# Where the vector engine's side work stands at the seams of a two-layer encoder: sums, weight splits, transposes and the loads of x

## The chip, the cores and the metric

The kernel runs on one core of a Trainium2 chip. The core has a matrix engine (TensorE, PE in the profile; PEld is its loading of the stationary operand), a vector engine (VectorE, DVE), an activation engine (ScalarE, ACT), GpSimd (POOL) and a queue engine that only issues transfers (SyncE, SP). The metric is the device time of one execution in microseconds, the median of several runs; lower is better.

## The reference

Two encoder layers over 256 tokens of width 1024, float32. Each layer has three sub-layers: a SwiGLU FFN of width 2816, a mixer (a gated MLP with 128-token position mixing in layer 0, chunked attention in layer 1), and a second FFN. A vector c gives per sub-layer a shift, a scale and a gate. Keys and values of the attention are projected once, from x behind layer 0.

```python
mod = (silu(c) @ w_ada[l] + b_ada[l])            # 9 vectors of 1024 per layer
h = x * (1 + scl[i]) + shift[i]
y = swiglu(h, gu, down)                          # or gmlp_mixer, or attention
x = layer_norm(ALPHA * x + w * gate[i] * y, g, b)
# behind layer 0: hkv = x * (1 + mkv[1]) + mkv[0];  k, v = hkv @ w_kv
```

## The kernel before

**Tiling.** The 256 tokens are two tiles of 128 rows, t = 0 and 1. Weights come in units of 128 rows by 1024 columns (512 KB). A product runs over its units in passes: a pass takes all units for tile 0, the next all for tile 1 (`gemm_pass`, L307). So a unit is consumed at two places, and only in tile 0's pass is a new one needed at each step.

**Splits.** Every float32 operand is split in two: ScalarE rounds it to `hi` (L214), VectorE makes `lo` = raw - hi (L224). A product is three matmuls per 512 columns: hi by hi (L278), lo by hi (L279) and hi by lo of the activations (L281). For the weights `hi`, `lo` are units; the activations' halves are called `hh`, `hl` for h (modulated x) and `th`, `tl` for an FFN's or mixer's inner values.

**Sums.** The vectors of `mod` are not made by TensorE. For each of 20 vectors and each 128 outputs VectorE multiplies a 512 KB block of w_ada with c and sums it (L141, `column`): a load from `w_cols` and one vector instruction over 128x1024. Sixteen of them open the kernel; the other 144 are strewn between the rest by a rate: `step` sets pieces (ticks, sums per tick), `pump` (L182) adds credit, `run_sums` issues a sum when there is credit of 1, or 2 where a split was issued in the same tick; `need` issues those of a vector that is due.

**Order.** The order on each engine is the order in which the program is written; nothing is moved later. A clock of ticks serves for it: a unit of a pass is one tick (half a tick where a pass does one half of the columns), and `after(n, fn)` puts work off by n ticks (`tick`, L293). `tick` also makes units ahead (`prep`, L228): 6 units ahead (8 before a sub-layer's end), as far as 11 buffers allow; 6 buffers hold raw blocks, weights and sums alike, and SyncE issues a load when its buffer is free.

**Seam.** A sub-layer's last output product is done by halves of 512 columns: tile 0's two halves, then tile 1's. Behind each half `add_y` (L380) adds the gated result to X, BN_STATS follows, behind the second half the norm (`end_sublayer`, L443: statistics, a power on GpSimd, and L447 on X, two halves). Some ticks later `make_h` (L359) transposes the normalised X on TensorE (L364, `hp`), ScalarE modulates it (L352, four instructions, and the cast L326), and VectorE makes `hl` (L329). For tile 0 this falls into tile 1's passes, for tile 1 into tile 0's first pass of the next sub-layer. Behind the second FFN of layer 0, h is made twice, for the next FFN and for K and V. There are five seams: behind FFN, gMLP, FFN of layer 0, FFN and attention of layer 1.

**Start.** `first_gu_part` (L486) does the first two blocks of the first FFN from a transposed copy of x. X itself is wanted first at the first residual; it is loaded by `load_small` (L118), called behind that part, before the third block's weights.

Of the kernel before, what the change touches and what calls it, by code (L numbers as in the profile page):

```python
# [14 lines left out]
P = 128  # L15
D = 1024
SEQ = 256
NT = SEQ // P
# [21 lines left out]


LAG_A = 3
LAG_H = 4
LAG_H2 = 2
LAG_R = ((12, 16), (12, 16))
LAG_S = 1
LAG_HL = 2
# [19 lines left out]
def encoder_kernel(ctx, tc, a, out):  # L67
    nc = tc.nc
# [8 lines left out]
    bigp = pool("bigp", N_BIG)  # L77
# [34 lines left out]
    def load_first():  # L112

        nc.sync.dma_start(out=bcol, in_=a["b_cols"])
        for sl in (slice(0, N_MODS, 2), slice(N_MODS, None)):
            nc.gpsimd.tensor_scalar(bcol[:, sl], bcol[:, sl], 1.0, None, op0=ALU.add)

    def load_small():  # L118
        for t in range(NT):
            nc.sync.dma_start(out=X[t], in_=a["x"][t * P:(t + 1) * P, :])  # L120
        nc.sync.dma_start(out=lncols, in_=a["lncols"])
        nc.sync.dma_start(out=bs_sb, in_=a["b_sT"])
        nc.sync.dma_start(out=wsT, in_=a["w_sT"])
        nc.gpsimd.memset(wsT[CH:P, :, 0:CH], 0.0)
# [54 lines left out]
    sums = [(key, j) for key in SUMS for j in range(KD)]  # L179
    ada = {"rate": [(0.0, 0.0)], "credit": 0.0}  # L180

    def pump(n):  # L182

        left, rate = ada["rate"][0]
        ada["credit"] = min(ada["credit"] + n * rate, 3.0)
        if len(ada["rate"]) > 1:
            ada["rate"][0] = (left - n, rate)
            if left - n <= 0:
                ada["rate"].pop(0)
# [38 lines left out]
    def prep(to, soon=0):  # L228

        free = min(now["freed"] + N_UNIT, len(stream))  # L230
        done_ = now["lo"]
        while now["lo"] < min(soon if now["lo"] > done_ else max(int(to), soon), free):
            prep_lo()
        while now["hi"] < min(now["lo"] + 1, free):
            prep_hi()
        return now["lo"] > done_
# [49 lines left out]
    def after(n, fn, early=False):  # L286
        late.append([n, fn, early])
# [2 lines left out]
        while late:  # L290
            late.pop(0)[1]()

    def tick(n, soon=0, quiet=False):  # L293
        for e in late:
            e[0] -= n
        due = [e for e in late if e[0] <= 0]
        for e in sorted(due, key=lambda e: not e[2]):
            late.remove(e)
            e[1]()
        now["at"] += n  # L300
        full = prep(now["first"] + now["ahead"] + now["n"] * now["at"] / now["ticks"], soon)
        pump(n)
        if not quiet:
            run_sums(full)
        load_gates()

    def gemm_pass(t, xs, units, nk, nb=2, accs=None, k0=0, cuts=HALVES, half=None):  # L307


        accs = accs or new_accs(nb)  # L310
        for ns in ([[s] for s in range(nb)] if half else [None]):
            share = (cuts[ns[0] + 1] - cuts[ns[0]]) / D if ns else 1
            for i, n in enumerate(units):
                mm_unit(accs, xs, get(n), i, nk, k0, ns, cuts)
                if t == NT - 1 and (not ns or ns[0] == nb - 1):
                    now["freed"] = n + 1
                tick(share, n + 3 if t == 0 else 0, half is not None and not (t == 1 and ns[0] == 0 and i > 4))
            if half:
                half(ns[0], accs[ns[0]])
        return accs  # L320
# [12 lines left out]
    def tiles4(hi, lo, n):  # L333
        return [(hi[:, q * P:(q + 1) * P], lo[:, q * P:(q + 1) * P]) for q in range(n)]
# [8 lines left out]
        split4(tp[:, :n * P], (hi[:, :n * P], lo[:, :n * P]),  # L343
               lambda: store.extend(tiles4(hi, lo, n)))

    def modulated(tp, A, B, js, p, tag, store):

        w = len(js) * P
        hf = sgp.tile([P, 512], F32, tag="sg", name=nm("hf"))
        for i, j in enumerate(js):  # L350
            sl = slice(i * P, (i + 1) * P)
            nc.scalar.activation(hf[:, sl], tp[:, sl], AF.Identity,  # L352
                                 bias=B[:, j:j + 1], scale=A[:, j:j + 1])
        hi = p.tile([P, 512], F32R, tag=tag, name=nm("hh"))
        lo = p.tile([P, 512], F32R, tag=tag, name=nm("hl"))
        split4(hf[:, :w], (hi[:, :w], lo[:, :w]),
               lambda: store.extend(tiles4(hi, lo, len(js))), LAG_HL)

    def make_h(t, half, mods_):  # L359

        js = range(half * 4, half * 4 + 4)
        tp = pt.tile([P, 512], F32, tag="pt", name=nm("hp"))
        for i, j in enumerate(js):
            nc.tensor.transpose(tp[:, i * P:(i + 1) * P], X[t][:, j * P:(j + 1) * P], ident)  # L364
        for A, B, p, tag, store in mods_:
            modulated(tp, A, B, js, p, tag, store[t])

    def affine(scl, shift, ln):

# [73 lines left out]
    def end_sublayer(t, stats, ln, nxt):  # L443

        mu, rs = stats.rstd()
        for x_ in pieces(X[t], HALVES):
            nc.vector.tensor_scalar(x_, x_, mu, rs, op0=ALU.subtract, op1=ALU.mult)  # L447
        hT[t] = []
        after(LAG_H, lambda: make_h(t, 0, nxt["mods"]))

        def second():
            make_h(t, 1, nxt["mods"])
            residual_affine(t, ln)
        after(LAG_H + LAG_H2, second)

    def last_y(t, gate, first, done, cuts=HALVES):

# [7 lines left out]
        return half  # L465


    def gu_out(t, accs, wd, aT):
        g, u = accs if wd == 512 else (accs[0][:, :wd], accs[0][:, wd:])
        sg = sgp.tile([P, 512], F32, tag="sg", name=nm("sg"))  # L470
        nc.scalar.activation(sg[:, :wd], g, AF.Silu)  # L471

        def second():
            av = ap_.tile([P, 512], F32, tag="a", name=nm("a"))
            nc.vector.tensor_tensor(av[:, :wd], u, sg[:, :wd], op=ALU.mult)  # L475
            after(LAG_A, lambda: transpose_split(av, wd // P, bigp, "b", aT[t]))
        after(LAG_S, second)

    def gu_part(part, aT):
# [6 lines left out]
    def first_gu_part(w_gu, part, aT):  # L486
# [96 lines left out]
        w = second()  # L583
        prep(1)
        for t in range(NT):
            gu_out(t, accs[0][t], 512, aT)
        matmuls(1, KD - 1, w)
        tick(2, 3)
        for t in range(NT):
            gu_out(t, accs[1][t], 512, aT)  # L590

    class Later:

# [325 lines left out]
    def step(ln, *rate):  # L919

        ada["rate"] = list(rate)
        nxt = {}
        return lambda t, stats: end_sublayer(t, stats, ln, nxt), nxt

    def final(t, stats):
        mu, rs = stats.rstd()
        g, b = lnrow[5]
        for c0, c1 in zip(ENDS[t], ENDS[t][1:]):
# [2 lines left out]
            nc.vector.scalar_tensor_tensor(x_, x_, rs, b[:, c0:c1], op0=ALU.mult, op1=ALU.add)  # L931
            nc.sync.dma_start(out=out[t * P:(t + 1) * P, c0:c1], in_=x_)

    ffn_stream(0, 0, PARTS1, 2)
    gmlp_stream()
    ffn_stream(0, 1, PARTS2)
# [2 lines left out]
    ffn_stream(1, 1, PARTS2)  # L939

    with tc.manual_schedule(engines={ET.SP, ET.PE, ET.DVE, ET.Activation, ET.Pool}):
        done, nxt = step(0, (20, 0.5), (0, 0.32))
        ffn(0, 0, (0, 2), done, next_affine(0, nxt, ((0, 4), (0, 3))), PARTS1, start=load_small)
        done, nxt = step(1, (0, 0.2))
        gmlp((0, 5), done, next_affine(1, nxt, ((0, 7), (0, 6))))
        done, nxt = step(2, (0, 0.33))
        ffn(0, 1, (0, 8), done, next_affine(2, nxt, ((1, 1), (1, 0)), (("kv", 1), ("kv", 0))), PARTS2)
        done, nxt = step(3, (0, 0.24))
        ffn(1, 0, (1, 2), done, next_affine(3, nxt, ((1, 4), (1, 3))), PARTS3)
        done, nxt = step(4, (0, 0.3))  # L950
        attention((1, 5), done, next_affine(4, nxt, ((1, 7), (1, 6))))
        step(5, (0, 0.4))
        ffn(1, 1, (1, 8), final, lambda: load_lnrow(5), PARTS2, cuts=ENDS)


# [38 lines left out]
```

## Time and profile before

| what | value |
|---|---|
| time, median of 3 runs | 1076.14 us (1076.09 to 1076.45) |
| the profiled execution | 1077.01 us, span 1075.2 us |
| TensorE busy | 1035.3 us, 96% |
| VectorE busy | 858.3 us, 80% |
| ScalarE busy | 503.9 us, 47% |
| mean granted TensorE clock | 0.988 |
| DMA moved | 285.75 MB, mean 266 GB/s |

How to read it: the matrix engine is busy in nearly the whole span, and the chain of work that ended last is its matmuls for 79%. So time is where it is not busy, and where its granted clock is below 1; both are seen in windows of the span, and the waits of the matrix engine name who ended them. The other engines' shares are averages over stages; what counts of them is whether they are in time at the places where the matrix engine waits.

### The profile page before, as it was taken

The page shows a single profiled execution, that of the slowest core. Times are in us where ns is not written, and L with a number is a line of the kernel's source. Part 1 is how long each engine was busy: PE and PEld are TensorE (multiplying, and loading weights), DVE is VectorE, ACT ScalarE, POOL GpSimd, SP SyncE. Part 2 cuts the span into 40 slices and gives each one's busy share as a digit, 9 for nine tenths or more (in the row PEclk, how much of TensorE's full clock was granted, in tenths as well). Part 3 has the DMA queues.
Part 4 walks back from the last instruction along what each step waited for, and adds up shares of the span by engine and source line. Part 5 has one row for each costly group of instructions (what it writes and reads, how often), then busy time and mean ns, then how long its engine had stood idle before and what let it go on. Part 6 is the DMA issues. An engine that isn't in the chain of part 4 may idle for free.

```text
span 1075.2 us, 13494 instructions
## 1 busy us (share of the span) xinstructions
PE 1035.3 (96%) x4774; PEld 847.3 (79%) x4774; DVE 858.3 (80%) x1224; ACT 503.9 (47%) x710; POOL 18.9 (2%) x41
## 2 busy tenths in 40 slices
PE   8989999898999899999979999999899989999996
PEld 6768888777888788888858888888787778888886
DVE  6898978999998899887778977878867877754545
ACT  4554444455433644443456444445456645443430
POOL 0000000001000000000000000000000000000000
PEclk9999999999999999999999999999999999999999
DMA  9999999788778689989956888887887655666541
GB/s 354 381 370 359 342 315 315 264 258 291 277 267 281 205 293 323 341 298 321 351 175 230 303 280 282 285 313 250 272 308 227 204 181 173 196 195 185 175 150 39
DMA packets 111348, 285.75 MB, mean 266 GB/s; under 512 B 9904, under 2 KB 22832, under 8 KB 111280
## 3 DMA queue, kind: packets, MB, share of 16 engines
q1 hardware_dynamic: 105648, 279.62, 75.4%
q10 hardware_dynamic: 5440, 5.24, 1.6%
q8 instruction: 37, 0.61, 0.2%
q14 instruction: 31, 0.25, 0.1%
q0 software_dynamic: 192, 0.02, 0.0%
HBM read 283.78 MB, written 1.07 MB: 265 GB/s over the span
## 4 chain that ended last, share of the span: by engine, by line
PE 79%; DVE 9%; DMA 5%; ACT 3%; issue 3%; POOL 1%; POOLq 0%; SPq 0%; DVEq 0%; ACTq 0%
PE acc L278 24%; PE acc L279 24%; PE acc L281 24%; DVE lo L224 3%; PE tp L340 2%; DVE raw L141 2%; DMA raw<-w_cols 2%; DMA raw<-ffn_gu 1%; PE sc L822 1%; ACT hi L214 1%; DMA bin<-b_in 1%; DVE st L407 1%; PE ob L874 1%; ACT hf L352 1%; DVE gy L389 1%
## 5 line engine op out<-in xcount | busy, mean ns | idle before, releaser
L224 DVE TENSOR_TENSOR lo<-raw,hi 128x1024 fp32r<-128x1024 f32 x328 | 393.2, 1220 | 25.9 <-ACT hi L214 25.4
L214 ACT CAST hi<-raw 128x1024 fp32r<-128x1024 f32 x328 | 335.1, 1050 | 158.9 <-DMA raw<-ffn_gu 58.8
L278 PE MATMUL acc<-hi,hh 128*128 128x512 f32 x864 | 346.5, 401 | 0.0
L279 PE MATMUL acc<-lo,hh 128*128 128x512 f32 x864 | 340.6, 394 | 3.6 <-DVE lo L224 3.5
L281 PE MATMUL acc<-hi,hl 128*128 128x512 f32 x864 | 274.8, 393 | 5.9 <-DVE hl L329 5.9
L141 DVE CUSTOM_DVE_ANT_0 raw<-raw,c_row,bcol 128x1024 f32<-128x1024 f32 x160 | 202.9, 1279 | 7.4 <-DMA raw<-w_cols 5.4
L281 PEld LDWEIGHTS acc<-hi,hl 128*128 128x128 f32 x864 | 163.9, 190 | 42.6 <-DVE hl L329 7.6
L279 PEld LDWEIGHTS acc<-lo,hh 128*128 128x128 f32 x864 | 164.4, 190 | 37.1 <-DVE lo L224 4.8
L278 PEld LDWEIGHTS acc<-hi,hh 128*128 128x128 f32 x864 | 164.4, 190 | 34.6 <-issue 1.7
L278 PE MATMUL acc<-hi,th 128*128 128x512 f32 (+1 forms) x432 | 167.2, 388 | 0.0
L279 PE MATMUL acc<-lo,th 128*128 128x512 f32 (+1 forms) x432 | 164.2, 382 | 0.0
L281 PE MATMUL acc<-hi,tl 128*128 128x512 f32 (+1 forms) x432 | 142.9, 382 | 0.0
L326 ACT CAST th<-tp 128x512 fp32r<-128x512 f32 (+1 forms) x56 | 31.0, 556 | 158.9 <-PE tp L340 158.9
L281 PEld LDWEIGHTS acc<-hi,tl 128*128 128x128 f32 x432 | 80.6, 188 | 16.1
L279 PEld LDWEIGHTS acc<-lo,th 128*128 128x128 f32 x432 | 81.3, 188 | 14.9
L278 PEld LDWEIGHTS acc<-hi,th 128*128 128x128 f32 x432 | 81.2, 188 | 14.9
L329 DVE TENSOR_TENSOR tl<-tp,th 128x512 fp32r<-128x512 f32 (+1 forms) x56 | 36.1, 650 | 61.3 <-ACT th L326 61.2
L352 ACT ACTIVATE hf<-hp,B,A 128x128 f32<-128x128 f32 x96 | 36.0, 455 | 84.5 <-PE hp L364 84.5
L475 DVE TENSOR_TENSOR a<-acc,sg 128x512 f32<-128x512 f32 (+1 forms) x48 | 30.8, 645 | 42.7 <-ACT sg L471 42.7
L389 DVE TENSOR_TENSOR gy<-acc,gate 128x512 f32<-128x512 f32 (+1 forms) x49 | 33.1, 675 | 21.6 <-PE acc L281 21.5
L471 ACT ACTIVATE sg<-acc 128x512 f32<-128x512 f32 (+1 forms) x48 | 26.7, 560 | 49.7 <-PE acc L281 49.4
L340 PE MATMUL tp<-ident,a 128*128 128x128 f32 x176 | 27.4, 277 | 3.8 <-DVE tl L329 3.8
(101 smaller groups left out, 620.3 us busy)
## 6 DMA issues: line engine op xcount, KB each, us to landing
raw<-w_cols SPq DMA_DIRECT2D x160, 512.0 KB, 5.3
raw<-ffn_gu SPq DMA_DIRECT2D x160, 512.0 KB, 5.3
raw<-ffn_down SPq DMA_DIRECT2D x88, 512.0 KB, 4.8
raw<-w_in SPq DMA_DIRECT2D x32, 512.0 KB, 5.6
raw<-ffn_gu SPq DMA_DIRECT2D x32, 256.0 KB, 4.4
raw<-w_out SPq DMA_DIRECT2D x16, 512.0 KB, 5.1
raw<-w_kv SPq DMA_DIRECT2D x16, 512.0 KB, 5.7
raw<-w_q SPq DMA_DIRECT2D x8, 512.0 KB, 4.6
```

What stands on the lines that cost most here:

```text
L141: nc.vector.tensor_tensor_reduce(out=raw, in0=raw, in1=c_row, scale=1.0, scalar=bcol[:, ci, j:j + 1], op0=ALU.mult, op1=ALU.add, accum_out ...
L214: nc.scalar.copy(hi, raw)
L224: nc.vector.tensor_tensor(lo, raw, hi.bitcast(F32), op=ALU.subtract)
L278: nc.tensor.matmul(acc, lhsT=xh, rhs=wh[:, sl], start=k == 0, stop=False)
L279: nc.tensor.matmul(acc, lhsT=xh, rhs=wl[:, sl], start=False, stop=False)
L281: nc.tensor.matmul(acc, lhsT=xl, rhs=wh[:, sl], start=False, stop=k == nk - 1)
L326: nc.scalar.copy(hi, src)
L329: nc.vector.tensor_tensor(lo, src, hi.bitcast(F32), op=ALU.subtract)
L340: nc.tensor.transpose(tp[:, q * P:(q + 1) * P], src[:, q * P:(q + 1) * P], ident)
L352: nc.scalar.activation(hf[:, sl], tp[:, sl], AF.Identity, bias=B[:, j:j + 1], scale=A[:, j:j + 1])
L389: nc.vector.tensor_tensor(tmp, acc[:, :w], mods[gate][:, sl], op=ALU.mult)
L475: nc.vector.tensor_tensor(av[:, :wd], u, sg[:, :wd], op=ALU.mult)
```

## The change

The sums no longer run inside the passes that are done by halves, and these passes give no credit for them; the credit is capped at 2 rather than 3; the rates have pauses at each sub-layer's start and are higher behind these. In tile 1's passes by halves, units are made only at the steps 1, 3 and 5 of each half. The transposes of X stand 4.5 (tile 0) and 5 ticks (tile 1) behind the norm rather than 4, and the second modulated copy's `hl` 1.5 ticks behind the first's. In the first two blocks the transposes of the inner values come 5 and 6 ticks later rather than 3. X and the small operands are loaded 12, 18 and 40 ticks into the first FFN's later part.

```diff
-LAG_H = 4
+LAG_H = (4.5, 5)
...
+    def load_x(t):
+        nc.sync.dma_start(out=X[t], in_=a["x"][t * P:(t + 1) * P, :])
+
     def load_small():
-        for t in range(NT):
-            nc.sync.dma_start(out=X[t], in_=a["x"][t * P:(t + 1) * P, :])
         nc.sync.dma_start(out=lncols, in_=a["lncols"])
...
-    def pump(n):
+    def pump(n, quiet):
 
         left, rate = ada["rate"][0]
-        ada["credit"] = min(ada["credit"] + n * rate, 3.0)
+        if not quiet:
+            ada["credit"] = min(ada["credit"] + n * rate, 2.0)
...
-    def tick(n, soon=0, quiet=False):
+    def tick(n, soon=0, quiet=False, split=True):
...
-        full = prep(now["first"] + now["ahead"] + now["n"] * now["at"] / now["ticks"], soon)
-        pump(n)
+        full = split and prep(now["first"] + now["ahead"] + now["n"] * now["at"] / now["ticks"], soon)
+        pump(n, quiet)
...
-                tick(share, n + 3 if t == 0 else 0, half is not None and not (t == 1 and ns[0] == 0 and i > 4))
+
+                tick(share, n + 3 if t == 0 else 0, half is not None,
+                     half is None or t == 0 or (i % 2 == 1 and i < 6))
...
-    def modulated(tp, A, B, js, p, tag, store):
+    def modulated(tp, A, B, js, p, tag, store, lag):
...
-               lambda: store.extend(tiles4(hi, lo, len(js))), LAG_HL)
+               lambda: store.extend(tiles4(hi, lo, len(js))), lag)
...
-        for A, B, p, tag, store in mods_:
-            modulated(tp, A, B, js, p, tag, store[t])
+        for i, (A, B, p, tag, store) in enumerate(mods_):
+            modulated(tp, A, B, js, p, tag, store[t], LAG_HL + 1.5 * i)
...
-        after(LAG_H, lambda: make_h(t, 0, nxt["mods"]))
+        after(LAG_H[t], lambda: make_h(t, 0, nxt["mods"]))
...
-        after(LAG_H + LAG_H2, second)
+        after(LAG_H[t] + LAG_H2, second)
...
-    def gu_out(t, accs, wd, aT):
+    def gu_out(t, accs, wd, aT, lag=LAG_A):
...
-            after(LAG_A, lambda: transpose_split(av, wd // P, bigp, "b", aT[t]))
+            after(lag, lambda: transpose_split(av, wd // P, bigp, "b", aT[t]))
...
-            gu_out(t, accs[0][t], 512, aT)
+            gu_out(t, accs[0][t], 512, aT, 5 + t)
...
+    def start():
+        for lag, fn in ((12, lambda: load_x(0)), (18, lambda: load_x(1)), (40, load_small)):
+            after(lag, fn)
...
-        done, nxt = step(0, (20, 0.5), (0, 0.32))
-        ffn(0, 0, (0, 2), done, next_affine(0, nxt, ((0, 4), (0, 3))), PARTS1, start=load_small)
-        done, nxt = step(1, (0, 0.2))
+        done, nxt = step(0, (6, 0), (16, 0.55), (0, 0.38))
+        ffn(0, 0, (0, 2), done, next_affine(0, nxt, ((0, 4), (0, 3))), PARTS1, start=start)
+        done, nxt = step(1, (4, 0), (16, 0.3), (24, 0), (0, 0.34))
...
-        done, nxt = step(2, (0, 0.33))
+        done, nxt = step(2, (4, 0), (16, 0.5), (0, 0.34))
...
-        done, nxt = step(3, (0, 0.24))
+        done, nxt = step(3, (4, 0), (16, 0.45), (0, 0.24))
...
-        done, nxt = step(4, (0, 0.3))
+        done, nxt = step(4, (4, 0), (0, 0.4))
...
-        step(5, (0, 0.4))
+        step(5, (2, 0), (0, 0.8))
```

The same number of sums, splits and matmuls is issued. On VectorE, behind the norm of tile 0 at the first seam (X_105 is tile 0, X_106 tile 1; `raw_1787` belongs to a sum, two more sums stand ahead of it; `gy` opens the residual), the kernel before has:

```order
L141 ISA raw_1787,mod_1786<-raw_1787,c_row,bcol 128x1024
L141 ISA mod_1786 128x1
L389 TENSOR_TENSOR gy_1790<-acc_1614,gate_936 128x512
L394 TENSOR_TENSOR X_106<-X_106,gy_1790 128x512
L407 BN_STATS st_1740<-X_106 128x6
L224 TENSOR_TENSOR lo_1801<-raw_1797,hi_1799 128x1024
L224 TENSOR_TENSOR lo_1810<-raw_1806,hi_1808 128x1024
L224 TENSOR_TENSOR lo_1819<-raw_1815,hi_1817 128x1024
L329 TENSOR_TENSOR hl_1784<-hf_1778,hh_1783 128x512
L224 TENSOR_TENSOR lo_1842<-raw_1838,hi_1840 128x1024
L329 TENSOR_TENSOR hl_1836<-hf_1830,hh_1835 128x512
L224 TENSOR_TENSOR lo_1861<-raw_1847,hi_1849 128x1024
```

The residual of tile 1's second half follows. Of the changed kernel, from the norm of tile 0 (first row):

```order
L451 TENSOR_SCALAR X_105<-X_105,mv_1741,rs_1743 128x512 x2
L393 TENSOR_TENSOR gy_1773<-acc_1617,gate_986 128x512
L398 TENSOR_TENSOR X_106<-X_106,gy_1773 128x512
L411 BN_STATS st_1748<-X_106 128x6
L226 TENSOR_TENSOR lo_1800<-raw_1796,hi_1798 128x1024
L226 TENSOR_TENSOR lo_1812<-raw_1802,hi_1804 128x1024
L333 TENSOR_TENSOR hl_1791<-hf_1785,hh_1790 128x512
L226 TENSOR_TENSOR lo_1840<-raw_1814,hi_1816 128x1024
L393 TENSOR_TENSOR gy_1852<-acc_1618,gate_986 128x512
...
L451 TENSOR_SCALAR X_106<-X_106,mv_1856,rs_1858 128x512 x2
L333 TENSOR_TENSOR hl_1835<-hf_1829,hh_1834 128x512
```

The sums are gone from between, three `lo` stand where five stood, and the second `hl` has moved behind the norm of tile 1.

On SyncE, behind the first two blocks of the first FFN (`ffn_gu` and `ffn_down` are weights, `w_cols` a sum's block), before:

```order
L132 DMA raw_576<-ffn_gu 128x2x512
L120 DMA X_105<-x 128x1024
L120 DMA X_106<-x 128x1024
L121 DMA lncols<-lncols 128x96
L122 DMA bs_sb<-b_sT 128x8
L123 DMA wsT<-w_sT 128x1024
L132 DMA raw_604<-ffn_gu 128x2x512
L132 DMA raw_616<-ffn_gu 128x2x512
L132 DMA raw_621<-w_cols 128x1024
L132 DMA raw_648<-ffn_gu 128x2x512
L132 DMA raw_678<-ffn_gu 128x2x512
L132 DMA raw_682<-w_cols 128x1024
```

And in the changed kernel, from the third block's last weights on:

```order
L133 DMA raw_622<-ffn_gu 128x2x512
L133 DMA raw_634<-ffn_gu 128x2x512
L133 DMA raw_654<-ffn_down 128x1024
L133 DMA raw_683<-ffn_down 128x1024
L133 DMA raw_704<-w_cols 128x1024
L133 DMA raw_716<-ffn_down 128x1024
L133 DMA raw_732<-w_cols 128x1024
L133 DMA raw_743<-ffn_down 128x1024
L133 DMA raw_753<-w_cols 128x1024
L119 DMA X_105<-x 128x1024
```

X, the small operands and two blocks of sums stand no longer among the third block's weights; the first tile of X is loaded behind five weights of the next product.

On VectorE behind the last seam (attention to the last FFN), from the norm of tile 1, before:

```order
L447 TENSOR_SCALAR X_106<-X_106,mv_7674,rs_7676 128x512 x2
L329 TENSOR_TENSOR hl_7718<-hf_7712,hh_7717 128x512
L224 TENSOR_TENSOR lo_7746<-raw_7665,hi_7668 128x1024
L329 TENSOR_TENSOR hl_7744<-hf_7738,hh_7743 128x512
L224 TENSOR_TENSOR lo_7766<-raw_7748,hi_7751 128x1024
L475 TENSOR_TENSOR a_7785<-acc_7682,sg_7775 128x512
```

And in the changed kernel:

```order
L451 TENSOR_SCALAR X_106<-X_106,mv_7636,rs_7638 128x512 x2
L333 TENSOR_TENSOR hl_7615<-hf_7609,hh_7614 128x512
L142 ISA raw_7652,mod_7216<-raw_7652,c_row,bcol 128x1024
L142 ISA mod_7216 128x1
L226 TENSOR_TENSOR lo_7661<-raw_7622,hi_7624 128x1024
L142 ISA raw_7673,mod_7216<-raw_7673,c_row,bcol 128x1024
L142 ISA mod_7216 128x1
L226 TENSOR_TENSOR lo_7682<-raw_7663,hi_7665 128x1024
L142 ISA raw_7708,mod_7216<-raw_7708,c_row,bcol 128x1024
L142 ISA mod_7216 128x1
L226 TENSOR_TENSOR lo_7717<-raw_7684,hi_7687 128x1024
L333 TENSOR_TENSOR hl_7706<-hf_7700,hh_7705 128x512
```

Between the splits of the last FFN's first pass there are now sums that were done earlier in the kernel before.

## Rows read from the trace of the kernel before

**Rows 1.** Windows: length, busy of PE, PEld, DVE, ACT, POOL, clock, DMA share, GB/s.

```profile
50.00:75.00 25.00, 21.15 (x94) 16.98 (x93) 22.01 (x29) 16.33 (x22) 0.52 (x1) 0.93 1.00 375
250.00:275.00 25.00, 22.16 (x91) 17.95 (x90) 24.57 (x37) 11.66 (x14) 2.98 (x2) 0.93 0.89 299
350.00:375.00 25.00, 21.79 (x96) 17.32 (x95) 22.42 (x34) 14.84 (x27) 1.13 (x2) 0.93 0.65 204
400.00:425.00 25.00, 25.00 (x113) 20.65 (x112) 24.71 (x35) 9.86 (x10) 0.00 (x0) 1.00 0.91 311
550.00:558.00 8.00, 5.47 (x23) 3.86 (x21) 5.74 (x8) 7.75 (x14) 0.00 (x0) 1.00 0.66 210
558.00:575.00 17.00, 11.68 (x45) 9.56 (x45) 12.55 (x21) 9.18 (x22) 1.13 (x2) 0.80 0.56 177
750.00:775.00 25.00, 21.53 (x97) 17.45 (x96) 21.98 (x32) 13.87 (x24) 1.11 (x3) 0.93 0.79 267
```

**Rows 2.** Waits of PE: for whom, us in total, times, longest.

```profile
PE hp L364 <- DVE X L447: 15.0, 5, 5.3
PE acc L281 <- DVE hl L329: 5.9, 4, 2.5
PE acc L279 <- DVE lo L224: 3.5, 2, 2.8
```

**Rows 3.** Timeline of PE: start, us, instruction, and idle before it with its releaser.

```profile
67.12 1.76 PE L340 MATMUL tp<-ident,a 128*128 128x128 f32 x8 [3.85 <-DVE tl L329]
...
265.50 0.79 PE L279 MATMUL acc<-lo,hh 128*128 128x512 f32 x1 [2.84 <-DVE lo L224]
...
359.11 0.73 PE L281 MATMUL acc<-hi,hl 128*128 128x512 f32 x2 [0.52 <-DVE hl L329]
...
366.63 0.66 PE L364 MATMUL hp<-ident,X 128*128 128x128 f32 x4 [2.69 <-DVE X L447]
...
553.13 0.74 PE L281 MATMUL acc<-hi,hl 128*128 128x512 f32 x2 [2.53 <-DVE hl L329]
```

**Rows 4.** Timeline of DVE at the first seam.

```profile
197.27 1.28 DVE L141 CUSTOM_DVE_ANT_0 raw<-raw,c_row,bcol 128x1024 f32<-128x1024 f32 x1
...
200.89 0.69 DVE L389 TENSOR_TENSOR gy<-acc,gate 128x512 f32<-128x512 f32 x1
...
202.95 3.48 DVE L224 TENSOR_TENSOR lo<-raw,hi 128x1024 fp32r<-128x1024 f32 x3
...
206.34 0.68 DVE L329 TENSOR_TENSOR hl<-hf,hh 128x512 fp32r<-128x512 f32 x1
...
209.85 0.68 DVE L389 TENSOR_TENSOR gy<-acc,gate 128x512 f32<-128x512 f32 x1
...
213.11 1.00 DVE L447 TENSOR_SCALAR X<-X,mv,rs 128x512 f32<-128x512 f32 x2 [0.69 <-POOL rs L415]
```

**Rows 5.** Timeline of PE at the first seam and in the FFN after the second.

```profile
198.25 0.60 PE L364 MATMUL hp<-ident,X 128*128 128x128 f32 x4
...
422.63 0.39 PE L279 MATMUL acc<-lo,hh 128*128 128x512 f32 x1
...
423.99 0.39 PE L279 MATMUL acc<-lo,hh 128*128 128x512 f32 x1
```

**Rows 6.** Timeline of ACT at the first and at the third seam.

```profile
201.00 2.94 ACT L214 CAST hi<-raw 128x1024 fp32r<-128x1024 f32 x3
...
545.85 1.50 ACT L352 ACTIVATE hf<-hp,B,A 128x128 f32<-128x128 f32 x4
...
547.91 2.94 ACT L214 CAST hi<-raw 128x1024 fp32r<-128x1024 f32 x3
```

**Rows 7.** Timeline of DVE in the FFN after the second seam.

```profile
420.66 2.36 DVE L224 TENSOR_TENSOR lo<-raw,hi 128x1024 fp32r<-128x1024 f32 x2
```

**Rows 8.** Loads of X on SP; and of the page's DMA issues, us to landing last.

```profile
50.65 1.07 SPq L120 DMA_DIRECT2D X<-x  x2
...
raw<-ffn_gu SPq DMA_DIRECT2D x160, 512.0 KB, 5.3
```

More of the change, by code (lines that the diff above doesn't have):

```diff
@@ L589, in first_gu_part @@
         for t in range(NT):
-            gu_out(t, accs[1][t], 512, aT)
+            gu_out(t, accs[1][t], 512, aT, 5 + t)
     class Later:
```

## Prediction

> **What bounds the kernel now.** I read the busy time by windows first. TensorE is busy without a break in most of the run; most of what it loses lies in a few windows: 50:75, 250:275, 350:375, 550:558, 558:575 and 750:775 each show 2.5 to 5.3 us without a matmul, and all but 550:558 a granted clock below 1 [rows 1]. The waits of TensorE say for whom: 15.0 us in five waits of the transposes `hp` for the normalised X, 5.9 us in four waits of the third product for `hl`, 3.5 us in two waits for a weight's `lo` [rows 2], and one of 3.85 us of the transposes `tp` [rows 3]. That is 28.3 us. The reader is to see that nearly all of it lies at the five seams between sub-layers, and that in each case VectorE is named.
>
> The clock adds to it. A granted share of 0.93 over 25 us is 1.75 us of lost matmul time, 0.80 over 17 us is 3.4; four windows of the one and one of the other make 10.4 us [rows 1]. Pauses of 2.69 us and more lie in those windows; the pause of 2.53 us that ends at 553.13 [rows 3] has a clock of 1.00 up to 558 [rows 1]. The levels are 2.4 and 1.2 GHz: behind the pauses the engine runs some microseconds at the lower one. So 28.3 + 10.4 = 38.7 us is all that this change could win; outside these places a unit of weights (six matmuls) takes 423.99 - 422.63 = 1.36 us [rows 5], and nothing in the change alters that.
>
> Why VectorE is late at a seam: in the first one three sums stand between the norm of tile 0 and the residual of tile 1, from 197.27 to 200.89, 1.21 us each; then three splits of 1.13, two `hl` with two more splits (206.34 to 209.85, so 0.63 for an `hl`), and only then the residual of the second half, whose norm ends 4.26 us later at 214.11 [rows 4]. TensorE had finished that half before 205 (the transposes at 198.25 [rows 5] and 6.2 us, worked out below), so VectorE was 5 us late.
>
> **The change part by part.** In all I call T1 the end of tile 1's first half at the last output product, T2 the end of its second. TensorE takes 4 x 1.36 + 2 x 0.4 = 6.2 us between them (eight half units and two groups of transposes, whose 0.60 [rows 5] holds a drain; 0.4 is my estimate).
>
> *Loads put off.* The two X loads and three small ones (1.6 MB) no longer stand ahead of the third block's weights [rows 8], nor do two of the sums. At the 375 GB/s of that window, whose DMA share is 1.00 [rows 1], 1.6 MB is 4.3 us, and the `tp` wait there 3.85 [rows 3]. The transposes `tp` also stand two or three units later. I take the 3.85 us and its 1.75 of clock as gone, but for 0.3 at a buffer. Bounds: 0 to 2.5 us left. X still comes long before its first use, between other weights; its two loads cost those 2.8 us of transfer, hidden by the units made ahead. On GpSimd the zeroing of a block of wsT moves with its load and holds that queue until it lands; behind it comes only the next gate's row, far from its use. One more sum stands before the last product of the first sub-layer: 0 to 1.2, I take 0.4.
>
> *Seams 1, 2, 5 (one modulated copy).* The transposes of tile 0 come half a unit after T1, at T1 + 0.7. ScalarE's casts start 201.00 - 198.25 = 2.75 us behind that, and the first takes 0.98 [rows 5, 6]: T1 + 4.4. The order has lo, lo, hl, lo before the residual: 3 x 1.13 + 0.63 = 4.0, so it starts at T1 + 8.4 = T2 + 2.2, against about T2 + 5 before. The norm's second half ends 4.26 later, at T2 + 6.5, the first half 0.5 earlier; the transposes of tile 1 now stand five units behind T2, at 6.8. So all five `hp` waits (15.0) go. What is late next is the second `hl` of tile 0, now behind the norm: T2 + 7.1, wanted after four units and four matmuls at T2 + 6.4. It costs 0.7 at each of the three seams, 2.1 in place of the waits for `hl` there. Bounds 0 to 4.5 in all.
>
> *Seam 3 (two copies, one for K/V).* ScalarE does another four activations and a cast first, 547.91 - 545.85 = 2.06 us [rows 6], and the order has a further `hl`: the residual starts at T2 + 4.9, `hl` is there at T2 + 9.8, TensorE waits 3.4. That is over 2.69, so I add 1.75 of clock: 5.2 in place of the 2.53 and 5.3 of the two windows and 3.4 of clock, 11.2 [rows 1, 3]. Bounds 1 to 8. Seam 4's first product runs on the K/V copy made long before, so it has no such wait.
>
> *Fewer splits in tile 1's pass.* They are put off, not saved. Behind each seam VectorE has two splits and one `hl` more to do, 2.9 us, and TensorE comes earlier. In the gMLP after seam 1: the wait of 0.7 (3.5 less 2.84) grows by 2.9 and by 2.5 (TensorE's saved waits), and shrinks by 3.0 (earlier start): 3.1, less the pauses VectorE had there itself, 0 to 2. I take 2.2, bounds 1.1 to 3.1. The 2.84 at 265.50 goes with its 1.75: three sums fewer (3.6) stand before that split. In the gMLP's last third two sums more stand among seven splits: 0 to 2.4, I take 1.0.
>
> In the FFN after seam 2 the split ready at 423.02 is wanted at 423.99 [rows 5, 7], and VectorE is busy 24.71 of 25 us there [rows 1]. The order up to that split has two splits, one sum and one `hl` more: 4.1. TensorE comes 0.52 + 2.69 + 1.75 - 0.7 = 4.2 earlier [rows 1, 3], VectorE starts 3.0 earlier, slack 0.97: 4.3 late, less the 2.58 us that VectorE had free in 350:375. Bounds 1.7 to 4.3; I take 3.4, spread over two units, so no clock term. After seam 3 the same sum gives 0 to 1, I take 0.3.
>
> *Sums moved into the last sub-layer.* VectorE goes there with sum, lo, sum, lo, sum, lo, hl behind the norm: 3 x 1.21 + 3 x 1.13 + 0.63 = 7.65, from T2 + 7.1 to 14.7; tile 1 wants that `hl` at 8 x 1.36 + 0.8 + 0.9 + 0.7 = 13.3. That is 1.5; bounds 0.5 to 3.
>
> **The sum.** Lost again: 0.3 + 0.4 + 2.1 + 5.2 + 2.2 + 1.0 + 3.4 + 0.3 + 1.5 = 16.4. Won: 38.7 - 16.4 = 22.3. The profiled execution took 1077.0 us (span 1075.2 and 1.8 around it), 0.9 over the median of 1076.1: 1077.0 - 22.3 - 0.9 = 1053.8, said as 1054.
>
> The clock is the loosest of these terms: pauses of 2.53 and 2.69 us, close in length, went without and with a drop [rows 1, 3]. [...]
>
> **Rivals.**
> A, the work behind the seams is hidden: VectorE's former pauses (2.58 us in one window alone) take the put-off splits, and only seam waits (2.1 and 5.2) and 0.3 remain. 38.7 - 7.6 = 31.1: 1045. For it: earlier starts let it fill those pauses. Against it: 24.71 of 25 in 400:425.
> B, VectorE takes the place of the seams: all upper bounds, 0.5 + 1.2 + 2.1 + 3.1 + 2.4 + 4.3 + 5.2 + 1 + 3 = 22.8, and the clock falls twice more, 3.5. Gain 12.4: 1064. For it: the sums and splits are the same in number, so whatever leaves the seams is done elsewhere.
> C, the change doesn't do what it says: the `hp` waits come from the chain residual to norm, not from the sums, and stay (15.0, with 6.9 of clock). The terms elsewhere come all the same (9.1). Gain 38.7 - 21.9 - 9.1 = 7.7: 1068. Against it: the three sums and two splits before it are plainly late work, and the transposes move.
> D, slower than before: with fewer splits only six of the next eight units are ready at T2, and the loads of the rest are issued later. A unit that lands late stops TensorE at each seam. The median from issue to landing is 5.3 us [rows 8]; the seventh unit is wanted at about T2 + 8.2 and its split then takes 1 + 1.1 us. The change is slower from 7.7 us per seam on (38.7 / 5, a 6 us pause and 1.75 of clock), which takes landings of about 11 us: 1078 and more. Against it: that is twice the median, and the windows with seams have the lowest DMA shares, 0.56 to 0.79 [rows 1].
>
> **How the numbers follow.** Forecast 0.50, A 0.20, B 0.20, C 0.04, D 0.04, no change 0.02. The range 1043 to 1066 takes A and B in and leaves out C, D and the far ends. A measurement here tells about 0.2%, 2.2 us, from no change. Faster: 0.50 + 0.20 + 0.20 + 0.04, less a little: 0.93; same 0.03; slower 0.04.
>
> **What would show it.** In the profile after: no wait of `hp` for the norm over 0.5 us; waits for `hl` of 0.5 to 1 at seams 1, 2 and 5 and near 3.4 at seam 3 with the clock below 1; no pause at 60 to 68; waits of the second product for `lo` in the gMLP and, near 400 to 425, of 2 to 4 us. I am wrong if `hp` still waits, or if waits for `lo` pass 12 us in total (then B), or are absent (then A).

## The result, and the profile after

| | before | after |
|---|---|---|
| median, us | 1076.12 (1075.67 to 1076.45, 4 runs) | 1062.99 (1062.69 to 1063.64, 4 runs) |
| ratio after to before | | 0.9879 (0.9862 to 0.9896) |
| profiled span, us | 1075.2 | 1060.9 |
| TensorE busy, us | 1035.3 | 1030.3 |
| VectorE busy, us | 858.3 | 856.8 |
| mean granted clock | 0.988 | 0.996 |

The kernel is 13.1 us faster; 22.3 were forecast. The time lies in the range, close to the 1064 of rival B, and not at the forecast of 1054. The two profiled executions lie 14.3 us apart in span, as the one before is 0.9 us above its median. Below I compare kernels by their ratio to the kernel before as run beside them, because its median on the chips of the experiments was 1076.8 to 1077.8. The changed kernel was timed on the first occasion alone, so differences from it of 2 to 4 us are less sure than the intervals look.

The waits of TensorE after (whom for, us in total, times, longest):

```profile
PE tp L344 <- DVE a L479: 8.8, 7, 2.3
PE acc L281 <- DVE lo L226: 5.1, 7, 2.0
PE acc L283 <- DVE hl L333: 3.9, 6, 2.1
```

Against [rows 2]: no wait of `hp` is left of 15.0 us, those for `hl` fell from 5.9 to 3.9, those for a weight's `lo` rose from 3.5 to 5.1. New is the first row: the transposes `tp` of an FFN's product wait for that product, `a`, which VectorE makes late. The prediction has no such term.

Windows after, to be read against [rows 1] (length, busy of PE, PEld, DVE, ACT, POOL, clock, DMA share, GB/s):

```profile
50.00:75.00 25.00, 25.00 (x119) 20.37 (x118) 24.28 (x30) 18.56 (x24) 0.00 (x0) 1.00 0.96 355
100.00:150.00 50.00, 49.59 (x223) 40.75 (x222) 44.49 (x58) 22.10 (x24) 0.52 (x1) 1.00 0.98 358
375.00:400.00 25.00, 23.04 (x105) 18.51 (x104) 24.40 (x36) 10.40 (x14) 0.58 (x1) 1.00 0.92 321
575.00:600.00 25.00, 21.66 (x99) 17.36 (x98) 24.83 (x37) 12.66 (x16) 0.58 (x1) 1.00 0.93 328
750.00:775.00 25.00, 25.00 (x120) 20.71 (x119) 24.56 (x33) 14.04 (x23) 0.00 (x0) 1.00 0.92 327
```

The seam windows are full and at full clock. TensorE now loses time some 20 to 40 us behind seams 2 and 3 (375:400, 575:600), where VectorE is busy for 24.4 and 24.8 of 25 us.

Where the time went, stage by stage: for each of the 328 splits of weights I read in both timelines when TensorE first uses it; the difference is how far the changed kernel is ahead. A number in brackets is that of the split at which the stage ends. The forecast column is the prediction's terms of that stage.

| stage (until split) | forecast, us | measured, us |
|---|---|---|
| start to seam 1 (49) | 5.6 - 0.3 - 0.4 = 4.9 | 3.1 (5.4 ahead at 81 us, then 2.3 lost) |
| seam 1 and gMLP (97) | 8.4 - 0.7 - 2.2 - 1.0 = 4.5 | 4.1 |
| seam 2 and FFN (160) | 5.0 - 0.7 - 3.4 = 0.9 | 0.3 (4.5 ahead, then 4.2 lost) |
| seam 3 and FFN (200) | 11.25 - 5.2 - 0.3 = 5.75 | 2.2 (8.1 ahead, then 5.9 lost) |
| seam 4 (240) | 5.2 | 5.2 |
| seam 5 and FFN (end) | 3.2 - 0.7 - 1.5 = 1.0 | -0.7 (3.9 ahead, then 4.6 lost) |
| sum | 22.3 | 14.2 |

What was off is thus what is lost again behind seams 3 and 5, and before seam 1. TensorE's timeline at and behind seam 3:

```profile
545.15 0.74 PE L283 MATMUL acc<-hi,hl 128*128 128x512 f32 x2 [2.06 <-DVE hl L333]
...
551.70 0.73 PE L283 MATMUL acc<-hi,hl 128*128 128x512 f32 x2 [0.78 <-DVE hl L333]
...
564.40 0.66 PE L344 MATMUL tp<-ident,a 128*128 128x128 f32 x4 [1.50 <-DVE a L479]
...
578.21 0.66 PE L344 MATMUL tp<-ident,a 128*128 128x128 f32 x4 [2.25 <-DVE a L479]
...
585.44 0.41 PE L344 MATMUL tp<-ident,a 128*128 128x128 f32 x2 [1.08 <-DVE a L479]
```

And VectorE there, its products and sums:

```profile
563.65 0.69 DVE L479 TENSOR_TENSOR a<-acc,sg 128x512 f32<-128x512 f32 x1 [2.81 <-ACT sg L475]
564.26 1.27 DVE L142 CUSTOM_DVE_ANT_0 raw<-raw,c_row,bcol 128x1024 f32<-128x1024 f32 x1
...
568.53 1.28 DVE L142 CUSTOM_DVE_ANT_0 raw<-raw,c_row,bcol 128x1024 f32<-128x1024 f32 x1
...
571.47 1.27 DVE L142 CUSTOM_DVE_ANT_0 raw<-raw,c_row,bcol 128x1024 f32<-128x1024 f32 x1
...
575.13 1.28 DVE L142 CUSTOM_DVE_ANT_0 raw<-raw,c_row,bcol 128x1024 f32<-128x1024 f32 x1
...
577.47 0.68 DVE L479 TENSOR_TENSOR a<-acc,sg 128x512 f32<-128x512 f32 x1
```

Four sums stand between two products `a`, 13.8 us apart; in the kernel before there were two sums, and the products were 10.8 us apart (576.54 and 587.36). The rate there is now 0.45 per tick, in place of 0.24.

### The profile page after: what moved, and what is told of

Same layout as the page of the kernel before. It is cut to its first block, busy times and chain, and to the rows that moved or that the text cites. A ratio compares the mean times of both kernels' runs of the same rounds, so it can differ in the third digit from the quotient of the medians.

```text
span 1060.9 us, 13486 instructions
## 1 busy us (share of the span) xinstructions
PE 1030.3 (97%) x4774; PEld 839.6 (79%) x4774; DVE 856.8 (81%) x1224; ACT 506.1 (48%) x710; POOL 18.9 (2%) x41
## 4 chain that ended last, share of the span: by engine, by line
PE 68%; DVE 16%; DMA 6%; issue 5%; ACT 3%; SPq 0%; POOL 0%; POOLq 0%; DVEq 0%; ACTq 0%
PE acc L280 20%; PE acc L283 20%; PE acc L281 19%; DVE lo L226 6%; DVE raw L142 4%; DMA raw<-w_cols 3%; PE tp L344 2%; PE acc L530 1%; PE acc L532 1%; PE acc L534 1%; ACT hf L356 1%; PE sc L826 1%; ACT hi L216 1%; DMA raw<-ffn_down 1%; DMA raw<-ffn_gu 1%
## 5 line engine op out<-in xcount | busy, mean ns | idle before, releaser
L283 PEld LDWEIGHTS acc<-hi,hl 128*128 128x128 f32 x864 | 161.5, 188 | 42.0 <-DVE hl L333 7.9
```

The costliest lines, as they stand in the source:

```text
L283: nc.tensor.matmul(acc, lhsT=xl, rhs=wh[:, sl], start=False, stop=k == nk - 1)
```

## The experiments

Rival causes: the sums (crowded behind the seam), the splits (put off behind it), the place of `tp`, and, at the start, the DMA engines. The expectations call a tick a half-step.

**Undoing one part each.** `tp` later:

```diff
-                gu_out(t, accs, wd, aT)
+                gu_out(t, accs, wd, aT, 6 if wd == 512 else LAG_A)
```

> The changed kernel with the transposes tp of each 512 wide gated product put off from 3 to 6 half-steps behind it. Theory 1 (only the place of the transposes in TensorE's queue is wrong): the seven tp waits, 8.8 us, go: 1054.2. Theory 2 (VectorE has no time left there): TensorE can gain only what the splits had in hand behind each wait, by the trace 0.06 us after seam 2, 1.8 after seam 3 and all 2.0 after seam 5, the rest comes back as waits for lo: 3.8 us, 1059.2. Theory 3 (VectorE sets the time throughout): no gain, 1063.

Ratio 0.9854 (0.9840 to 0.9868), 2.7 us below the changed kernel, but the two intervals overlap and the profiled spans are 1060.8 and 1060.9 us.

```profile
PE tp L344 <- DVE a L479: 6.4, 4, 4.5
PE acc L281 <- DVE lo L226: 5.7, 8, 2.0
```

Fewer waits, but one grew to 4.5 us: that for the product of 256 columns, whose transposes kept their place. It ends when VectorE has done that `a` (585.33 plus 0.41); ahead of it stand sums and three splits that TensorE first uses 6 to 11 us after they are ready. The clock falls at two waits (0.93 in 225:250 and in 575:600), where it did not after the change. The lag alone isn't the cause. Theory 2 is nearest, though the wait stays with `a` and doesn't move to `lo` as it said.

The splits back:

```diff
-                     half is None or t == 0 or (i % 2 == 1 and i < 6))
+                     True)
```

> The changed kernel with the splits of weights in the pass of tile 1 made as before, the sums still paused. Theory 1 (the prediction's steps): two splits more, 2.3 us, stand before the residual of tile 1; the transposes hp had 1.2 to 1.7 us in hand (0.2 at seam 4), so they wait about 0.6 to 1.1 at four seams and 2.1 at the fourth, 5 in all; behind the seams VectorE has 2.3 us less to do, which gives 2.3 back at each of seams 2, 3 and 5 and at the gMLP, 7 in all: 1061 (1059 to 1064). Theory 2 (the fewer splits are what frees the seams): hp waits and clock drops return, 10 us or more slower, 1073.

Ratio 0.9999 (0.9988 to 1.0010): the whole gain is gone, and my theory 1 is refuted.

```profile
PE acc L283 <- DVE hl L333: 12.9, 6, 4.3
PE tp L344 <- DVE a L479: 5.7, 4, 2.3
PE acc L281 <- DVE lo L226: 4.2, 6, 2.0
PE hp L368 <- DVE X L451: 2.0, 1, 2.0
```

Theory 2 has the size and the falls of the clock right (0.93 in 350:375, 0.86 in 550:575), but not the wait: it is `hl` that waits, since the splits stand ahead of it. And four of the seven `tp` waits stay, behind seams 2 and 3, the same to 0.01 us (0.87, 1.09, 1.50 and 2.25 us against 0.86, 1.10, 1.50 and 2.25), although no split is put off. So put-off splits don't make those 5.7 us. The other 3.1, at 585 and behind seam 5, are gone; whether by the splits' place or because TensorE comes later, this run doesn't tell.

The sums back (the old rates, the cap of 3 and the old condition for `quiet`; no pause at the start either):

```diff
-        if not quiet:
-            ada["credit"] = min(ada["credit"] + n * rate, 2.0)
+        ada["credit"] = min(ada["credit"] + n * rate, 3.0)
```

> The changed kernel with the old rule for the sums: not paused in the tile passes, the old rates and the old cap of 3. Theory 1 (the sums made the hp waits): two or three sums of 1.21 us come back ahead of the residual of tile 1, against 1.2 to 1.7 us in hand: hp waits of about 2 us at five seams, 10 in all, two clock drops of 1.6, and at the places behind the seams 2 to 5 us less of waits for the products: 1069 to 1073. Theory 2 (the later transposes and fewer splits alone had freed them): no hp wait over 0.5 us, 1058 to 1063, since the sums no longer crowd behind the seams.

Ratio 0.9842 (0.9829 to 0.9855): faster than the changed kernel, by about 4 us, although the pause at 66 us (3.4 us) is back. No `hp` wait returns, and the `tp` waits for `a` fall from 8.8 to 1.5. Theory 1, the prediction's, is refuted: with the fewer splits, the sums at the seam cost next to nothing there. Why is seen on VectorE at the first seam, first after, then with the sums back:

```profile
193.35 1.00 DVE L451 TENSOR_SCALAR X<-X,mv,rs 128x512 f32<-128x512 f32 x2 [0.75 <-POOL rs L419]
195.46 0.69 DVE L393 TENSOR_TENSOR gy<-acc,gate 128x512 f32<-128x512 f32 x1 [1.11 <-PE acc L283]
...
199.77 2.36 DVE L226 TENSOR_TENSOR lo<-raw,hi 128x1024 fp32r<-128x1024 f32 x2 [2.16 <-PE hp L368]
...
203.79 0.68 DVE L393 TENSOR_TENSOR gy<-acc,gate 128x512 f32<-128x512 f32 x1
```

```profile
196.63 1.00 DVE L450 TENSOR_SCALAR X<-X,mv,rs 128x512 f32<-128x512 f32 x2 [0.76 <-POOL rs L418]
197.55 1.28 DVE L142 CUSTOM_DVE_ANT_0 raw<-raw,c_row,bcol 128x1024 f32<-128x1024 f32 x1
...
198.75 1.28 DVE L142 CUSTOM_DVE_ANT_0 raw<-raw,c_row,bcol 128x1024 f32<-128x1024 f32 x1
...
199.96 1.28 DVE L142 CUSTOM_DVE_ANT_0 raw<-raw,c_row,bcol 128x1024 f32<-128x1024 f32 x1
...
207.22 0.68 DVE L392 TENSOR_TENSOR gy<-acc,gate 128x512 f32<-128x512 f32 x1
```

From the norm to the last residual it is 203.79 - 193.35 = 10.44 us without the three sums and 207.22 - 196.63 = 10.59 with them. Where they stood, VectorE waits 1.11 us for TensorE's half and 2.16 us for ScalarE, whose cast stands behind the modulation that waits for `hp`. The 3.6 us of sums were in a pause. In the kernel before it was 209.85 - 196.35 = 13.5 us [rows 4]: the 2.9 us are two splits and an `hl`, not the sums.

The kernel before had less of a pause there. Its first cast ended at 201.00 + 0.98 = 201.98 us and its first `lo` began at 202.95 [rows 4, 6], so without the sums that `lo` could have begun about 1.0 us earlier; this is an estimate from these rows. No run pauses the sums at the seams with all the splits and the old lags in place.

The lags of the transposes and of the second `hl` back:

```diff
-LAG_H = (4.5, 5)
+LAG_H = (4, 4)
...
-            modulated(tp, A, B, js, p, tag, store[t], LAG_HL + 1.5 * i)
+            modulated(tp, A, B, js, p, tag, store[t], LAG_HL)
```

> The changed kernel with the transposes of x and the hl of the second copy at their former places (lags 4 and 4, no 1.5 more for the second copy). Theory 1 (the later transposes are what the hp waits needed): tile 1's hp transposes come 1.36 us earlier; they had 1.2 to 1.7 us in hand at four seams and 0.2 at seam 4, so hp waits of up to 0.2 at four seams and 1.1 at seam 4, with tile 0's hl up to 0.7 us earlier: 1062 to 1065. Theory 2 (the lags carried a good part of the gain): hp waits of 2 us and clock drops return: 1068 or more.

Ratio 0.9919 (0.9898 to 0.9941), 4.3 us slower than the changed kernel, between the theories.

```profile
PE hp L368 <- DVE X L451: 11.0, 5, 5.5
PE acc L283 <- DVE hl L333: 0.3, 1, 0.3
```

The `hp` waits return (1.4 us at four seams, 5.5 at seam 3): theory 2, though with fewer clock drops than it has.

**One part alone, on the kernel before.** The fewer splits:

> The kernel before with the fewer splits in tile 1's pass alone. Theory 1 (from the two runs above: with the splits back the waits for hl return and the gain is gone, with the sums back all is kept): the fewer splits carry nearly all of the gain: the hl waits (5.9 us) and most of the hp waits go, the pause of 3.85 us at 63 us stays: 1062 to 1065. Theory 2 (the prediction's: the three sums of 1.21 us before the residual matter as much as the two splits): hp waits shrink by 2.3 us each, to 0.4, 3.0 and 1.2 at seams 2, 3 and 4, and two clock drops stay; behind the seams about 5 comes back: 1067 to 1069.

Ratio 0.9905 (0.9883 to 0.9926), 1066: between the theories. The `hp` waits shrink to 1.3 to 1.6 us at four seams, and at seam 3 one of 5.5 stays.

```profile
PE hp L365 <- DVE X L448: 11.3, 5, 5.5
PE tp L341 <- DVE tl L330: 4.3, 1, 4.3
PE acc L281 <- DVE hl L330: 0.3, 1, 0.3
```

The start part (X, small loads, the first `tp` later), and then that with 6 ticks without sums, `(6, 0), (16, 0.6), (0, 0.33)` in place of `(20, 0.5), (0, 0.32)`:

> The kernel before with the first part of the change alone: the X loads, the three small loads and the transposes of the first four products later. Theory 1 (the prediction's): the wait of 3.85 us and its 1.75 us of clock go, the loads are hidden later, 0.3 is lost: 5.3 us faster, 1070.8. Theory 2 (the transfers are only put off into a stretch where the DMA engines are full, 0.97 busy from 100 to 190 us after the change): half is given back as waits for lo and hi before the first seam, as TensorE's progress does between the two traces (6.5 us ahead at 63 us, 3.1 at 184): 3.1 us faster, 1073.0. Theory 3: all is given back, 1076.

> The kernel before with the start part of the change and its first 6 half-steps without sums. Theory 1 (at the start VectorE's sums, not the loads, hold the transposes; the loads alone gave about 3.4 us of median and nothing in TensorE's progress by 86 us): the pauses at 66 and 71 us go, 4 to 5 us ahead at 130 us, about 3 of it kept to the first seam: 1071 to 1073, 2 to 3 us below the run with the loads alone. Theory 2 (the loads did it): same as the loads alone within 1 us.

Ratios 0.9968 (0.9955 to 0.9980) and 0.9951 (0.9931 to 0.9970), not told apart by themselves. The traces tell them apart. With the loads alone the pause at 63 us goes, but

```profile
68.47 0.66 PE L341 MATMUL tp<-ident,a 128*128 128x128 f32 x4 [2.02 <-DVE tl L330]
...
72.19 1.12 PE L341 MATMUL tp<-ident,a 128*128 128x128 f32 x4 [0.84 <-DVE tl L330]
```

come 5 us later, with the clock drop, and at 87 us TensorE is 0.8 us behind the kernel before. With the pause of the sums as well TensorE does not wait there and is 3.9 ahead at 87 us, but only 0.3 at the end of that sub-layer: it loses most of this in three waits for `lo` (2.6 us), where ScalarE's casts wait 1.5 to 2.4 us each for loads of weights. So with the loads alone the profiled run has given all of it back by 87 us (theory 3 of the first text, though by waits for `tl`); with the sums paused too, most is given back before the first seam. At the start theory 1 of the second text holds: the sums hold the transposes. The pause of the sums without the later loads was not run, and where the loads' 3.4 us by the ratio come from, the profiled run doesn't show.

**Which sums cost.** The pause of the sums kept only at the start (otherwise as with the sums back; rates as just given):

> The changed kernel with the old rule and rates for the sums everywhere but in the first sub-layer, which has its first 6 half-steps without sums as in the changed kernel. Theory 1 (the pause at the start is worth 4.8 us, as TensorE's progress shows between the changed kernel and the one with the sums back, the pauses at the seams cost some): no pause at 66 us, and the rest as with the sums back: 3 to 5 us below that run, 1055 to 1057, so below the changed kernel by 6 to 8. Theory 2 (what is won at the start is given back before the first seam, where the DMA engines are 0.97 busy): 1059 to 1060, as with the sums back.

Ratio 0.9803 (0.9778 to 0.9828), 1054.6 us: theory 1 by the time, 0.4 us below its range. But of the 6.7 us between this profiled span and that with the sums back, 2.9 are there at the first seam; the rest comes behind it, where the program differs little, and is not shown to be the pause's. And the pauses at the seams kept, but no crowding behind them:

```diff
-        done, nxt = step(2, (4, 0), (16, 0.5), (0, 0.34))
+        done, nxt = step(2, (4, 0), (0, 0.38))
...
-        done, nxt = step(3, (4, 0), (16, 0.45), (0, 0.24))
+        done, nxt = step(3, (4, 0), (0, 0.28))
...
-        step(5, (2, 0), (0, 0.8))
+        step(5, (2, 0), (0, 0.4))
```

> The changed kernel, its sums still paused at the seams, but made up for evenly over the sub-layers behind seams 2, 3 and 5 and not in the first 16 half-steps (rates 0.38, 0.28, 0.4 in place of 0.5, 0.45, 0.8 there). Theory 1 (the sums crowded in those half-steps make the products a late, so the tp waits): of the 8.8 us of tp waits under 2 stay, no clock drop: 1055 to 1057. Theory 2 (the put-off splits make them): the tp waits stay within 2 us, 1061 to 1063. Theory 3 (the place of tp three half-steps behind the product makes them, whatever VectorE does): as theory 2, with VectorE idle before a.

Ratio 0.9816 (0.9798 to 0.9835), 1057.4 us.

```profile
PE acc L281 <- DVE lo L226: 7.4, 11, 2.0
PE acc L283 <- DVE hl L333: 3.4, 5, 2.1
PE tp L344 <- DVE a L479: 2.2, 2, 1.5
```

The waits for `a` go from 8.8 to 2.2 and 2.3 us come back as waits for `lo`: theory 1, if 0.4 us above its range. The pauses at the seams are still in this run, and its ratio is not told apart from the 0.9803 without them: what cost was the crowding behind the pauses. The wait of 1.5 us left is that behind ScalarE's `sg`:

```profile
553.39 1.51 ACT L356 ACTIVATE hf<-hp,B,A 128x128 f32<-128x128 f32 x4 [1.95 <-PE hp L368]
...
563.53 0.59 ACT L475 ACTIVATE sg<-acc 128x512 f32<-128x512 f32 x1
```

From the first of these to the second ScalarE has no pause: four modulations with their casts (the first line opens them), two of them second copies, and two casts of weights stand ahead of `sg`.

**What stands in the better version.** The second copy at seam 3 three ticks later, on the version with the pause at the start only:

```diff
+            def copy(A=A, B=B, p=p, tag=tag, store=store):
+                modulated(tp, A, B, js, p, tag, store[t], LAG_HL)
+            if i:
+                after(3, copy)
+            else:
+                copy()
```

> The run with the pause at the start only, and in it the second modulated copy at seam 3 (for K and V) made 3 half-steps after the first. Theory 1 (the prediction's step: ScalarE's second copy, 2.06 us, holds back the first copy's hl): the hl waits of 2.08 and 0.80 us at seam 3 go: 1051.5 to 1052.5. Theory 2 (VectorE's own order, splits before hl, sets them): the waits stay, 1054 to 1055.

Ratio 0.9773 (0.9755 to 0.9791), 1053.0 us: between the two ranges, and the interval overlaps with that of the version without it. The trace decides. The `hl` waits of 2.08 and 0.80 us at seam 3 fall to 0.22 each: theory 1, in the size the trace gives (TensorE is 2.5 us further ahead behind that seam, and the span 2.9 us shorter).

The gMLP's sums later, `(40, 0), (0, 0.34)` in place of `(0, 0.2)`, on the version with the pause at the start only; then half of them, `(40, 0.1), (0, 0.26)`, with the second copy later too:

> The run with the pause at the start only, and in it no sums in the first 40 half-steps of the gMLP, then 0.34 per half-step in place of 0.2. Theory 1 (VectorE's sums make the waits for lo there): the three waits of 1.00, 0.79 and 1.74 us go, up to 1 us comes back in the gMLP's last third: 1051 to 1053. Theory 2 (the put-off splits and the V work make them): two of the three stay, 1053 to 1055.

> The run with the second copy later, and in it half of the gMLP's sums moved from its first 40 half-steps to the rest (0.1, then 0.26, in place of 0.2). Theory 1 (VectorE has some time left in the gMLP's rest, as 19 sums later lost 7.6 us there and won 5): two of the three lo waits shrink, 1 to 2 us won and under 1 lost: 1051 to 1052.5. Theory 2 (VectorE has none left there; every sum moved costs at its new place what it gave at the old): the same within 0.7 us, 1052.5 to 1053.5.

The first: ratio 0.9816 (0.9799 to 0.9833), not told apart from the version without, though the profiled span is 2.6 us longer; both theories missed. The three waits go and TensorE is 5.2 us further ahead, but 7.6 us are lost in the gMLP's last third and at seam 2. The second: ratio 0.9735 (0.9715 to 0.9754), 1050.05 us, the best of all and below both ranges. Against the run before it, its trace is 2.0 us ahead in the gMLP, 1.3 until seam 4 and 0.1 at the end, so the trace does not account for the 0.4% between the two ratios, which were measured on different occasions. Theory 1 holds in the gMLP, theory 2 over the whole; what gives the rest stays open.

## Why the prediction was right and where it failed

The main step, that VectorE holds TensorE at the seams and that the change frees them, was right. The sum was not: by the table of stages it is 8.1 us too high, 3.6 behind seam 3, 1.8 before seam 1, 1.7 behind seam 5 and 1.0 in the two stages between. That the time lies in the range is in part luck: the range was drawn wide enough for rival B, and B's mechanism did not come.

The two waits that the fewer splits and the lags remove, side by side (TensorE's waits, us):

| kernel | splits in tile 1's pass | lags | sums at the seams | `hp` | `hl` |
|---|---|---|---|---|---|
| before | all | old | run | 15.0 | 5.9 |
| start part and pause on before | all | old | run | 14.3 | 6.7 |
| lags back | fewer | old | paused | 11.0 | 0.3 |
| fewer splits alone | fewer | old | run | 11.3 | 0.3 |
| splits back | all | later | paused | 2.0 | 12.9 |
| after | fewer | later | paused | 0 | 3.9 |
| sums back | fewer | later | run | 0 | 3.8 |

- *Won at the seams* (38.7 gross): right. All `hp` waits went, and with them the clock drops of [rows 1]. The step's cause was half right: splits and lags do it together. The lags without the fewer splits (the sums paused) turn `hp` waits into `hl` waits, the splits alone leave 11 us of `hp`. Pausing the sums changes neither by more than 0.3 us in the two pairs with fewer splits (of which one differs in the start part as well); a pair with all the splits was not run. "VectorE was 5 us late" [rows 4] was read with three sums as its first cause; that step failed, for they lay in a pause, all but about 1.0 us by the estimate above.
- *Seams 1, 2, 5*, 0.7 of `hl` each: 0.15, 0.17 and 0.16; right in kind, under a quarter of the size.
- *Seam 3*, 3.4 of `hl` and a clock drop, 5.2: the waits were 2.06 and 0.78, 2.8 in all, with the clock at 1.00. The cause, ScalarE's second copy, was right, as the run with it later shows. The clock term was not needed in this run.
- *gMLP after seam 1*, 2.2: 0.31 and 2.01, right; its last third, 1.0: 0.19 and 0.76, right. *FFN after seam 2*, 3.4: 4.2, of which 2.0 are `tp` and 0.67 `lo` waits; part of the rest is the transposes of x, which now come later. The size was near by luck: the prediction looked for 2 to 4 us of `lo` waits here, and the wait it did not have, `tp`, is the larger.
- *After seam 3* 0.3 and *last sub-layer* 1.5: the failed terms. Measured 5.9 and 4.6, with `tp` waits of 4.8 and 2.0 in them; the `hl` wait that the 1.5 stands for is there, with 0.61. The prediction looked for VectorE's lateness where a weight's `lo` or `hl` is wanted; most of these had 4 to 13 us in hand there. What was late first was `a`, wanted three ticks behind its product. And it counted sums ahead of splits and `hl` only, while a rate of 0.45 puts four sums between two products instead of two.
- *Loads put off*, 5.6 won and 0.7 lost: 5.4 ahead at 81 us, 3.1 at 184. (The 6.5 at 63 us, which one expectation names, counts transposes that the changed kernel makes only behind that.) So the gain was right and the loss 2.3. What the prediction put at nothing ("hidden by the units made ahead") is there: the DMA engines are 0.98 busy in 100:150, and before seam 1 ScalarE's cast, which a split needs, waits for a block of ffn_down, while TensorE waits 0.38 and 0.76 us at 182 and 183:

```profile
181.42 1.05 ACT L216 CAST hi<-raw 128x1024 fp32r<-128x1024 f32 x1 [2.73 <-DMA raw<-ffn_down]
```

  That the put-off loads make this loss is argued, not shown: no run has the changed kernel with the loads at their old place. And the gain at 63 us needs the pause of the sums.
- *Rivals.* B has the time but not the way: waits for `lo` are 5.1 us, far from its 12. Its 1064 isn't "all upper bounds" either: it takes 0.5, 2.1 and 5.2 where the bounds given are 2.5, 4.5 and 8; with these it comes to 1071. A is out. C's doubt, that the sums don't make the `hp` waits, was right where it was run, with the fewer splits; its conclusion, that these stay, was not. D is out: no wait for a unit's load at the seams.

## What to carry to other kernels

Before moving work out of an engine's queue, look whether the engine waits right behind it: work that stands in a pause is free there and costs where it is put. And when side work is put off, look in the queue it joins not only for the consumer that you know to be tight, but for whichever is wanted soonest behind its instruction. Undoing parts one at a time shows what a bundle hides: here one part of four, the sums paused at the seams and crowded behind them, worked against the rest, and without it the gain was 2.0% in place of 1.2%.

## What the runs showed of the hardware

Between 2.0 and 2.65 us, the length of a pause of TensorE did not decide on its clock in these runs. The wait for `lo` behind seam 1 was 2.01 us after and 2.00 with the sums back, after nearly the same matmuls; window 225:250 of the one, then of the other:

```profile
225.00:250.00 25.00, 22.68 (x99) 18.15 (x98) 23.81 (x34) 11.62 (x13) 1.46 (x1) 1.00 0.92 308
```

```profile
225.00:250.00 25.00, 23.00 (x94) 18.36 (x93) 23.16 (x33) 8.86 (x11) 0.00 (x0) 0.93 0.79 270
```

One went on at 2.4 GHz (1.00), the other fell for some microseconds to 1.2 GHz. With even rates the same wait (2.00 us) left the clock alone; with the products later or the splits back (2.01 us) it fell. The wait of 2.53 us at seam 3 of the kernel before [rows 3] left it alone, and in the run of the start part alone the same wait, again ending at 553.13, did not; window 550:562 of the one, then of the other:

```profile
550.00:562.00 12.00, 5.47 (x23) 3.86 (x21) 9.60 (x14) 7.75 (x14) 0.00 (x0) 1.00 0.65 204
```

```profile
550.00:562.00 12.00, 7.06 (x23) 4.98 (x21) 9.59 (x14) 7.73 (x14) 0.00 (x0) 0.86 0.60 202
```

In that same run a pause of 2.65 us left it alone (1.00 in 365:380). The Trainium skill, "TensorE: Matmul & The Clock Gate", section "What's actually happening", says "it's run-variable" of the number of slow matmuls at a kernel's start alone. That pauses of one length inside a kernel differ as well is what these traces show. So a forecast should give such pauses a share of a drop: the prediction's own drop at seam 3 (1.75 us) was one that did not come.
